# Second half's feed-forward input: 17 of 22 tile pairs as Strassen's 2x2 block product with blocks of 256 tokens, the operand normalised behind the merge

## The chip, the cores and the metric

The kernel runs on one core of a Trainium2 chip. The metric is the time of one execution in microseconds on the device; for the kernel before, the median of three runs is given. A core has TensorE (matmuls, in the profile PE, with its weight loads as PEld), VectorE (DVE), ScalarE (ACT), GpSimd (POOL) and SyncE (SP, which here only issues transfers). Each engine works off its own instructions in order and waits on semaphores for the others.

## What is computed

One decoder layer over 1024 tokens of width 1024, in float32: an RWKV-7 time mixing and an indexer-selected sparse attention, merged by sigmoid gates, then a SwiGLU feed-forward and a final RMSNorm. The part that matters here:

```python
merged = g_a * (y_a @ w_o_rwkv) + g_b * (y_b @ w_o_att)
h = h + merged @ w_out
z = rmsnorm(h, norm2_g) @ w_ffn_in          # 1024 -> 2 x 2816
z_gate, z_up = jnp.split(z, 2, axis=-1)
h = h + (jax.nn.silu(z_gate) * z_up) @ w_ffn_out
return rmsnorm(h, normf_g)
```

## The kernel before, in words

Activations lie transposed: 128 channels in the partitions, 512 tokens (one of two halves of the sequence) in the columns, 8 such tiles for the width of 1024. Every large product is made in three terms, to keep float32's precision: weight and activation are split into a high part, rounded to the PE's input type, and a low part, the rest (`split`, L113: ScalarE copies the high part, VectorE subtracts for the low one), and TensorE adds high x high, high x low and low x high. `mm3` (L135) does that for one output tile of 128 channels x 512 tokens: 8 steps along the width x 3 terms = 24 matmuls of 512 columns into one PSUM tile.

The feed-forward has 22 tile pairs: pair J gives 128 channels of the gate and the same 128 of the up branch, 48 matmuls. `ffn` (L1411) works in three groups of 8, 8 and 6 pairs; behind each group `ffn_out` (L1282) multiplies the group's result f by the output weights and adds it to the stream h, which lies in DRAM. In a pair `ffn_in` (L1254) multiplies both results by a row of one over the RMS per token (`row`), makes silu out of a tanh, multiplies gate and up, and splits the result into f's high and low part. The operand z is h times the norm's gain, without the row: so the products can start before the row is known, and the first pair is ordered (`mm3_late`, L1240) so that z's low part comes last.

What sets the order: TensorE's order is as written, by generators that yield a number of matmuls; `pump(n)` (L175) runs n matmuls of filler from the queue `fill`, and `run_over` (L199) runs a generator and pumps where it yields a negative number. All other engines' instructions are put in order by a scheduler at build time, and their waits follow from tiles and buffers. Weights come in tiles of 512 KB by SP's queue into three raw buffers (`wst`), are split (`weights`, L124) into `whi` and `wlo`, two buffers each.

Around the change the main program does the second half's `merge` (L1193: output projections, gates, `w_out`, h, sums of squares), with the last `ffn_out` of the first half as filler (144 matmuls, 40 of them inside the merge), then the second half's `ffn`, inside which the first half's final norm is placed (`norm_out`, L1313), then a closing stage (`finish_out`). `Rms.columns` sums the squares over the partitions by small matmuls, POOL takes a power, `Rms.spread` brings the result back to all partitions by four small matmuls, and `row` copies that from PSUM. PSUM has 3 tiles `acc` and 5 tiles `mix`; scratch tiles `tmp` are 4.

## Time and profile before

| | |
|---|---|
| median of 3 runs | 1733.7 us |
| lowest, highest | 1728.94, 1736.04 us |
| span of the profiled execution (the page gives no other time of it) | 1731.2 us |
| PE busy | 1700.7 us, 98% |
| DVE, ACT, POOL busy | 65%, 49%, 6% |
| second half's feed-forward to the closing stage | from 1358 to about 1697 us of the span |

In the profile a row of a group reads: line, engine, operation, tiles written <- tiles read, shape, count, then busy time and mean duration, then idle time of the engine before these rows with what ended it. In the chain and timeline views the first number is the start in us from the span's start, the second the duration. In the windows view each stretch has its length, then the busy time of PE, PEld, DVE, ACT and POOL with instruction counts, the granted TensorE clock, the DMA share and GB/s.

### The profile page before, as it was taken

What the parts mean: (1) busy time and instruction counts of PE and PEld (TensorE: products, weight loads), DVE (VectorE), ACT (ScalarE), POOL (GpSimd) and SP (SyncE); (2) the same over time, 40 slices, a digit from 0 to 9 for tenths busy, and PEclk for the clock granted to TensorE, in tenths of its full rate; (3) what the DMA queues carried; (4) which work ended last, traced back from release to release, by engine and by line L of the source; (5) the groups of instructions that cost most, each with busy time, mean ns of one, the idle gap of its engine ahead of it and who ended that gap; (6) DMA issues with size and microseconds to landing.
All of it is one profiled execution on the core that took longest, in us unless ns stands there. A gap on an engine that the chain in (4) does not pass through costs nothing.

```text
span 1731.2 us, 26658 instructions
## 1 busy us (share of the span) xinstructions
PE 1700.7 (98%) x10072; PEld 1405.5 (81%) x10072; DVE 1118.3 (65%) x2172; ACT 848.6 (49%) x1631; POOL 104.8 (6%) x127
## 2 busy tenths in 40 slices
PE   8999999999999998999999999999999999999998
PEld 6888888888778777878787888888888888888888
DVE  6789889866568567857776655535565564354364
ACT  6365998553554788655334355433334322232232
POOL 0000000010021101001100311000000000000001
PEclk9999999999999999999999999999999999999999
DMA  5542334536266536644343765164465344434442
GB/s 212 178 135 96 98 98 147 165 102 182 93 198 185 154 108 177 209 125 117 100 126 117 220 161 136 62 210 131 164 207 151 101 156 152 140 97 152 140 122 98
DMA packets 143282, 247.69 MB, mean 143 GB/s; under 512 B 49153, under 2 KB 71361, under 8 KB 143025
## 3 DMA queue, kind: packets, MB, share of 16 engines
q1 hardware_dynamic: 119072, 170.76, 32.2%
q10 hardware_dynamic: 16128, 48.60, 9.0%
q0 software_dynamic: 7952, 26.61, 5.8%
q8 instruction: 80, 1.31, 0.3%
q14 instruction: 50, 0.40, 0.1%
HBM read 192.92 MB, written 53.00 MB: 142 GB/s over the span
## 4 chain that ended last, share of the span: by engine, by line
PE 89%; DVE 5%; DMA 2%; ACT 2%; issue 1%; POOL 1%; SPq 0%; POOLq 0%; ACTq 0%; DVEq 0%
PE acc L140 22%; PE acc L145 22%; PE acc L141 22%; PE acc L158 3%; PE mix L1103 2%; PE mix L1079 2%; PE mix L944 2%; PE mix L1093 2%; DVE wlo L115 1%; PE mix L140 1%; PE mix L141 1%; PE mix L145 1%; PE acc L1247 1%; PE mix L829 1%; PE mix L699 1%
## 5 line engine op out<-in xcount | busy, mean ns | idle before, releaser
L115 DVE TENSOR_TENSOR wlo<-wst,whi 128x1024 fp32r<-128x1024 f32 (+1 forms) x221 | 268.8, 1218 | 270.3 <-PE acc L145 130.9
L114 ACT ACTIVATE whi<-wst 128x1024 fp32r<-128x1024 f32 (+1 forms) x221 | 231.7, 1049 | 228.5 <-PE acc L141 172.2
L140 PE MATMUL acc<-zhi,whi 128*128 128x512 f32 x672 | 264.7, 394 | 0.0
L141 PE MATMUL acc<-zlo,whi 128*128 128x512 f32 x672 | 262.0, 390 | 0.0
L145 PE MATMUL acc<-zhi,wlo 128*128 128x512 f32 x672 | 170.4, 392 | 0.0
L140 PEld LDWEIGHTS acc<-zhi,whi 128*128 128x128 f32 x672 | 126.2, 188 | 26.9 <-issue 1.7
L141 PEld LDWEIGHTS acc<-zlo,whi 128*128 128x128 f32 x672 | 126.3, 188 | 24.8
L145 PEld LDWEIGHTS acc<-zhi,wlo 128*128 128x128 f32 x672 | 124.7, 188 | 25.5 <-issue 0.7
L140 PE MATMUL acc<-u1hi,whi 128*128 128x512 f32 x320 | 128.4, 401 | 0.0
L141 PE MATMUL acc<-u1lo,whi 128*128 128x512 f32 x320 | 125.5, 392 | 0.0
L140 PE MATMUL acc<-u0hi,whi 128*128 128x512 f32 (+1 forms) x320 | 122.8, 386 | 0.0
L141 PE MATMUL acc<-u0lo,whi 128*128 128x512 f32 (+1 forms) x320 | 121.3, 382 | 0.0
L140 PE MATMUL acc<-fhi,whi 128*128 128x512 f32 x234 | 91.9, 393 | 0.1
L141 PE MATMUL acc<-flo,whi 128*128 128x512 f32 x234 | 91.2, 390 | 0.0
L114 ACT ACTIVATE fhi<-tmp 128x512 fp32r<-128x512 f32 x44 | 27.8, 631 | 114.5 <-DVE tmp L1279 114.5
L145 PE MATMUL acc<-u1hi,wlo 128*128 128x512 f32 x320 | 81.8, 395 | 0.0
L145 PE MATMUL acc<-u0hi,wlo 128*128 128x512 f32 (+1 forms) x320 | 78.6, 384 | 0.0
L1084 ACT ACTIVATE L<-L,mx 128x128 f32<-128x128 f32 (+7 forms) x64 | 49.6, 774 | 45.8 <-DVE mx L1081 45.4
L994 ACT ACTIVATE junkl<-kept,z 128x1024 int8<-128x1024 int16 (+1 forms) x64 | 69.4, 1084 | 4.7 <-DVE kept L963 4.4
L1276 ACT ACTIVATE tmp<-tmp 128x512 f32<-128x512 f32 x44 | 27.8, 631 | 88.8 <-DVE tmp L1275 88.8
L140 PEld LDWEIGHTS acc<-u1hi,whi 128*128 128x128 f32 x320 | 60.3, 189 | 12.7 <-issue 0.9
L140 PEld LDWEIGHTS acc<-u0hi,whi 128*128 128x128 f32 x320 | 60.2, 188 | 11.9 <-issue 0.4
(368 smaller groups left out, 3390.8 us busy)
## 6 DMA issues: line engine op xcount, KB each, us to landing
wst<-in_w_ffn_in SPq DMA_DIRECT2D x72, 512.0 KB, 3.7
wst<-in_w_in ACTq DMA_DIRECT2D x36, 512.0 KB, 4.5
wst<-in_w_in SPq DMA_DIRECT2D x27, 512.0 KB, 3.8
wst<-in_w_fo SPq DMA_DIRECT2D x25, 512.0 KB, 4.2
k<-d_k POOLq DMA_DIRECT2D x24, 512.0 KB, 8.2
h<-in_xT SPq DMA_DIRECT2D x32, 256.0 KB, 5.6
d_g<-tmp ACTq DMA_DIRECT2D x32, 256.0 KB, 3.6
tmp<-d_g SPq DMA_DIRECT2D x32, 256.0 KB, 3.6
```

The costliest lines, as they stand in the source:

```text
L114: A.activation(hi, x, AF.Copy)
L115: V.tensor_tensor(lo, x, hi.bitcast(F32), op=ALU.subtract)
L140: T.matmul(ps, whi[:, wk + k, :], ahi[:, ak + k, tok], start=k == 0, stop=False)
L141: T.matmul(ps, whi[:, wk + k, :], alo[:, ak + k, tok], start=False, stop=False)
L145: T.matmul(ps, wlo[:, wk + k, :], ahi[:, ak + k, tok], start=False, stop=k == nk - 1)
L158: T.matmul(ps, w[:, k, :], a[:, k, tok], start=k == 0 and j == 0, stop=k == nk - 1 and j == 2)
L944: T.matmul(ps[:, :w], iq[:, h, :], ik[:, i, c:c + w], start=i == 0, stop=i == 1)
L994: A.activation(junka[:, :n], y, AF.Sign, bias=z[:, i:i + 1], accum_out=cnt[:, i:i + 1])
L1079: T.matmul(ps[:, :w], q[bi // 2][:, e, bi % 2 * 128:bi % 2 * 128 + 128], k[:, i, e, c:c + w], start=i == 0, stop=i == 1)
L1084: A.activation(L[:, :n], L[:, :n], AF.Exp, scale=-1.0, bias=last, accum_out=sm[:, bi, e:e + 1])
L1093: T.transpose(ps[:, j * 128:(j + 1) * 128], L[:, (c + j) * 128:(c + j + 1) * 128], ident)
L1103: T.matmul(py[64 * e:64 * e + 64, bi * 128:(bi + 1) * 128], v[:, j, 64 * e:64 * e + 64], pts[e][j // 4][:, j % 4, :], start=j == b, stop=j ...
```

## The change

Pairs 3 to 19 of the second half are computed by a 2x2 block product with seven products instead of eight (Winograd's form of Strassen's scheme). The 2x2 block matrix of weights has the gate and the up tile as rows and the two halves of the width (512 each) as columns; that of z has the two halves of the width as rows and the two halves of the tokens (256 each) as columns. One product is 4 steps x 3 terms = 12 matmuls of 256 columns, so a pair has 84 of them instead of 48 of 512 columns.

- `operands` makes z with gain and row in it, behind the merge, splits it, and makes four sums and differences of z's blocks (t1 to t4) with their high and low parts, once for all pairs.
- `prepare` makes, for each pair, four sums of weight blocks (`raw`), and splits these, the gate tile and half of the up tile; its steps are written between the products of the pair ahead. `raw` and the split sums (`bhi`, `blo`) have two buffers each, in a new pool that lies where the first half's tiles lay.
- `pair` writes the seven products: three accumulate further in a PSUM tile after an engine has read it. The seventh product of a pair (`last_block`) is written after four products of the next pair, or at once at a group's end.
- The merge of the second half no longer makes z; sums of squares, row and z follow it, with the 104 matmuls of filler spread between. Pairs 0 to 2, 20 and 21 are as before, without the multiplication by the row. `norm_out` comes 50 matmuls into the feed-forward instead of 100.

In the program's new order, line numbers of helpers are two higher than before (L115 is L117). Three places. First, ScalarE between the merge and the feed-forward, before (L273 is the copy of the row, L114 with `whi` and 768 columns the filler's weights, with 1024 the feed-forward's):

```order
L114 ACTIVATE whi<-wst 128x1024 [waits DMAHW1_49,PE_49,Activation_49]
L114 ACTIVATE whi<-wst 128x1024 [waits DMAHW2_49,PE_49,Activation_49]
L273 ACTIVATE row<-mix 128x512 [waits PE_49]
L1276 ACTIVATE tmp<-tmp 128x512 [waits DVE_49]
L114 ACTIVATE whi<-wst 128x1024 [waits DMAHW3_49,PE_49,Activation_49]
L114 ACTIVATE fhi<-tmp 128x512 [waits DVE_49]
```

and now (L275 is the copy of the row, L248 the squares, L116 `zhi` the high part of z):

```order
L116 ACTIVATE whi<-wst 128x768 [waits DMAHW0_49,PE_49]
L248 ACTIVATE tmp<-h 128x512 [waits DVE_49]
L116 ACTIVATE whi<-wst 128x768 [waits DMAHW2_49,PE_49,Activation_49]
L275 ACTIVATE row<-mix 128x512 [waits PE_49]
L116 ACTIVATE zhi<-h 128x512 [waits DVE_49]
L248 ACTIVATE tmp<-h 128x512 [waits DVE_49]
L116 ACTIVATE whi<-wst 128x768 [waits DMAHW4_49,PE_49,Activation_49]
L116 ACTIVATE zhi<-h 128x512 [waits DVE_49] x2
```

The copy of the row stood behind the first pair's weights; it now stands behind the filler's third last weights, and z's high parts follow it.

Second, VectorE there, before (L1307 adds the filler's result, L247 the squares, L256 is the step of the norm, L1275 to L1279 work on the first pair's result):

```order
L1307 TENSOR_TENSOR h<-h,acc 128x512 [waits DMASW1_49]
L247 TENSOR_TENSOR sacc<-sacc,tmp 128x512 [waits Activation_49]
L256 TENSOR_SCALAR rs<-mix 128x4 [waits PE_49]
L115 TENSOR_TENSOR wlo<-wst,whi 128x1024 [waits DMAHW1_49,Activation_49]
L115 TENSOR_TENSOR wlo<-wst,whi 128x1024 [waits DMAHW2_49,DVE_49,Activation_49]
L1275 TENSOR_TENSOR tmp<-acc,row 128x512 [waits Activation_49]
L1277 SCALAR_TENSOR_TENSOR tmp<-tmp 128x512 [waits Activation_49]
L1278 SCALAR_TENSOR_TENSOR tmp<-acc,row 128x512 [waits DVE_49,PE_49]
L1279 TENSOR_TENSOR tmp<-tmp 128x512 [waits DVE_49]
```

and now (L1313 and L249 for the filler, L1436 multiplies h by gain and row):

```order
L258 TENSOR_SCALAR rs<-mix 128x4 [waits PE_49]
L1313 TENSOR_TENSOR h<-h,acc 128x512 [waits DMASW4_49]
L249 TENSOR_TENSOR sacc<-sacc,tmp 128x512 [waits Activation_49]
L117 TENSOR_TENSOR wlo<-wst,whi 128x768 [waits DVE_49,DMAHW2_49,PE_49,Activation_49]
L1436 SCALAR_TENSOR_TENSOR h<-h,par,row 128x512 [waits DMAHW7_49,Activation_49]
L1313 TENSOR_TENSOR h<-h,acc 128x512 [waits DMASW5_49]
L1436 SCALAR_TENSOR_TENSOR h<-h,par,row 128x512 [waits DMAHW1_49]
L117 TENSOR_TENSOR zlo<-h,zhi 128x512 [waits Activation_49]
L249 TENSOR_TENSOR sacc<-sacc,tmp 128x512 [waits Activation_49]
```

The multiplications by the row and z's low parts stand between the filler's own steps now, eight of each.

Third, VectorE in one pair, before (one pair's steps and the splits of two weight tiles):

```order
L115 TENSOR_TENSOR wlo<-wst,whi 128x1024 [waits DMAHW0_49,PE_49,Activation_49]
L1278 SCALAR_TENSOR_TENSOR tmp<-acc,row 128x512 [waits DVE_49]
L1279 TENSOR_TENSOR tmp<-tmp 128x512 [waits DVE_49]
L115 TENSOR_TENSOR flo<-tmp,fhi 128x512 [waits Activation_49]
L115 TENSOR_TENSOR wlo<-wst,whi 128x1024 [waits DMAHW4_49,PE_49,Activation_49]
L1275 TENSOR_TENSOR tmp<-acc,row 128x512
L1277 SCALAR_TENSOR_TENSOR tmp<-tmp 128x512 [waits Activation_49]
```

and now, from a pair's third product to its sixth (L1466 to L1469 are sums of weights for the next pair, L1521, L1535, L1542 take products out of PSUM, L1504 and L1505 belong to the last product of the pair ahead, L1537 is the gate, `wlo` and `blo` are low parts of the next pair's weights):

```order
L1521 TENSOR_TENSOR tmp<-tmp,mix 128x256 [waits PE_49,Activation_49]
L1468 TENSOR_TENSOR raw<-raw,wst 128x512 [waits DVE_49]
L1505 SCALAR_TENSOR_TENSOR tmp<-m_13456,tmp 128x256
L1469 TENSOR_TENSOR raw<-raw,wst 128x512 [waits DVE_49]
L117 TENSOR_TENSOR wlo<-wst,whi 128x1024
L117 TENSOR_TENSOR blo<-raw,bhi 128x1024 [waits PE_49,Activation_49]
L1504 SCALAR_TENSOR_TENSOR tmp<-mix,tmp 128x256
L1535 TENSOR_TENSOR tmp<-tmp,acc 128x256 [waits PE_49]
L117 TENSOR_TENSOR blo<-raw,bhi 128x1024 [waits Activation_49]
L117 TENSOR_TENSOR flo<-tmp,fhi 128x512 [waits Activation_49]
L1537 SCALAR_TENSOR_TENSOR tmp<-tmp 128x512 [waits Activation_49]
L1542 TENSOR_TENSOR m_13579<-mix,m_13579 128x256 [waits PE_49]
```

Between a result and the steps that wait for ScalarE stand splits of the next pair's weights.

The diff, without the kernel's unchanged helpers:

```diff
--- before.py
+++ after.py
@@ -25,6 +25,8 @@
 HT = 512
 NFF = 22
 GROUPS = [(0, 8), (8, 8), (16, 6)]
+BLOCKED = range(3, 20)
+HB = HT // 2
 TOPK = 256
 C1 = math.exp(-0.5)
 NEG = -3.0e38
@@ -1217,7 +1219,7 @@
         h = zp.tile([128, 8, HT], F32, tag="s0", name="h")
         load_x(half, h, range(8))
         sq = Rms(h)
-        zt = zhi, zlo = act_tiles(zp, "z", ("s1", "s3"))
+        zt = zhi, zlo = act_tiles(zp, "z", ("s1", "s3")) if half == 0 else (None, None)
         pss = []
         if half == 0:
             pss = [acc(), acc()]
@@ -1229,9 +1231,13 @@
                 ps = acc()
                 yield from mm3(ps, weights(ins["w_out"][d]), mt)
             V.tensor_tensor(h[:, d, :], h[:, d, :], ps, op=ALU.add)
-            A.activation(zhi[:, d, :], h[:, d, :], AF.Copy, scale=par[:, P_N2 + d:P_N2 + d + 1])
+            if half == 0:
+                A.activation(zhi[:, d, :], h[:, d, :], AF.Copy, scale=par[:, P_N2 + d:P_N2 + d + 1])
             SY.dma_start(d_h[half][d], h[:, d, :])
             sq.add(d)
+        if half == 1:
+            zs.append(sq)
+            return
         for d in range(8):
             V.scalar_tensor_tensor(zlo[:, d, :], h[:, d, :], par[:, P_N2 + d:P_N2 + d + 1],
                                    zhi[:, d, :].bitcast(F32), op0=ALU.mult, op1=ALU.subtract)
@@ -1417,6 +1423,170 @@
                 yield from ffn_out(half, zp, f, gi)
         kept.append(f)
+    def operands(zp, op, sq, row):
+        h = sq.h
+        z = zhi, zlo = act_tiles(zp, "z", ("s1", "s3"))
+        b = {(r, c): h[:, 4 * r:4 * r + 4, HB * c:HB * c + HB] for r in range(2) for c in range(2)}
+        ts = {i: tuple(op.tile([128, 4, HB], F32R, name=f"t{i}{n}") for n in ("hi", "lo")) for i in range(1, 5)}
+        def steps():
+            for k in range(8):
+                V.scalar_tensor_tensor(h[:, k, :], h[:, k, :], par[:, P_N2 + k:P_N2 + k + 1], row,
+                                       op0=ALU.mult, op1=ALU.mult)
+                split(zhi[:, k, :], zlo[:, k, :], h[:, k, :])
+                yield
+            x, y = b[0, 0], b[0, 1]
+            V.tensor_tensor(x, x, y, op=ALU.subtract)
+            split(*ts[1], x)
+            yield
+            V.tensor_tensor(y, b[1, 1], y, op=ALU.subtract)
+            for i, o in ((2, b[1, 1]), (4, b[1, 0])):
+                V.scalar_tensor_tensor(x, x, -1.0, o, op0=ALU.mult, op1=ALU.subtract)
+                split(*ts[i], x)
+                yield
+            split(*ts[3], y)
+            yield
+        return z, ts, steps()
+    def ffn_blocked(zp, z, ts, steps, wr, kept):
+        zb = {(r, c): tuple(x[:, 4 * r:4 * r + 4, HB * c:HB * c + HB] for x in z) for r in range(2) for c in range(2)}
+        def prepare(J, out):
+            hi, lo = (wr[0].tile([128, 5, 4, 128], F32R, tag=f"b{n}", name=f"b{n}", bufs=2) for n in ("hi", "lo"))
+            raw = wr[0].tile([128, 4, 4, 128], F32, tag="raw", name="raw", bufs=2)
+            def steps():
+                g, u = (raw_weights(ins["w_ffn_in"][2 * J + i]) for i in range(2))
+                for i, a, b in ((0, u[:, 0:4], u[:, 4:8]), (3, g[:, 0:4], u[:, 0:4])):
+                    V.tensor_tensor(raw[:, i], a, b, op=ALU.add)
+                    yield
+                V.tensor_tensor(raw[:, 1], raw[:, 0], g[:, 0:4], op=ALU.add)
+                V.tensor_tensor(raw[:, 2], raw[:, 1], g[:, 4:8], op=ALU.add)
+                yield
+                for i in (0, 2):
+                    split(hi[:, i:i + 2], lo[:, i:i + 2], raw[:, i:i + 2])
+                    yield
+                gs = weights(None, st=g, rush=False)
+                yield
+                split(hi[:, 4], lo[:, 4], u[:, 4:8])
+                w = [tuple(x[:, 4 * i:4 * i + 4] for x in gs) for i in range(2)]
+                out.extend(w + [(hi[:, i], lo[:, i]) for i in range(5)])
+                while True:
+                    yield
+            return steps()
+        def product(ps, w, a, opens=False):
+            (whi, wlo), (ahi, alo) = w, a
+            for k in range(4):
+                T.matmul(ps, whi[:, k, :], ahi[:, k, :], start=opens and k == 0, stop=False, skip_group_check=True)
+                T.matmul(ps, whi[:, k, :], alo[:, k, :], start=False, stop=False, skip_group_check=True)
+            for k in range(4):
+                T.matmul(ps, wlo[:, k, :], ahi[:, k, :], start=False, stop=k == 3, skip_group_check=True)
+        ready, nxt, prev = {}, [iter(())], []
+        def other(J):
+            if J in BLOCKED:
+                ready[J] = []
+                nxt[0] = prepare(J, ready[J])
+            else:
+                nxt[0] = iter(())
+        def last_block():
+            x, w, m5, t, j, f = prev.pop()
+            product(x, w, ts[4])
+            V.scalar_tensor_tensor(t[:, :HB], x, -0.5, t[:, :HB], op0=ALU.mult, op1=ALU.mult)
+            V.scalar_tensor_tensor(t[:, HB:], m5, -0.5, t[:, HB:], op0=ALU.mult, op1=ALU.mult)
+            split(f[0][:, j, :], f[1][:, j, :], t)
+        def pair(J, j, f, ends):
+            a11, a12, s1, s2, s4, s3, a22 = ready.pop(J)
+            x, y, p = mix()[:, :HB], acc()[:, :HB], mix()[:, :HB]
+            c, m5 = tmp(), wr[1].tile([128, HB], F32, tag="m5", name="m5", bufs=2)
+            product(x, a11, zb[0, 0], True)
+            A.activation(c[:, :HB], x, AF.Copy)
+            next(nxt[0], None)
+            yield 6
+            product(y, s1, ts[1], True)
+            A.activation(m5, y, AF.Copy)
+            next(nxt[0], None)
+            yield 6
+            product(p, a12, zb[1, 0], True)
+            V.tensor_tensor(c[:, :HB], c[:, :HB], p, op=ALU.add)
+            next(nxt[0], None)
+            yield 6
+            product(x, s2, ts[2])
+            A.activation(c[:, HB:], x, AF.Copy)
+            next(nxt[0], None)
+            yield 6
+            if prev:
+                last_block()
+                yield 6
+            t = tmp()
+            def low():
+                product(y, s4, zb[1, 1])
+                V.tensor_tensor(c[:, HB:], c[:, HB:], y, op=ALU.add)
+                A.activation(t, c, AF.Tanh, scale=0.5)
+                V.scalar_tensor_tensor(t, t, 1.0, c, op0=ALU.add, op1=ALU.mult)
+                next(nxt[0], None)
+            def high():
+                product(x, s3, ts[3])
+                V.tensor_tensor(m5, x, m5, op=ALU.add)
+                next(nxt[0], None)
+            for step in ((high, low) if ends else (low, high)):
+                step()
+                yield 6
+            for _ in range(2):
+                next(nxt[0], None)
+            prev.append((x, a22, m5, t, j, f))
+            if ends:
+                last_block()
+                yield 6
+        for gi, (g0, gn) in enumerate(GROUPS):
+            f = act_tiles(zp, "f", ("s2", "s0"))
+            for j in range(gn):
+                J = g0 + j
+                if J in BLOCKED:
+                    other(J + 1 if j < gn - 1 else -1)
+                    yield from pair(J, j, f, j == gn - 1 or J + 1 not in BLOCKED)
+                    continue
+                if J + 1 in BLOCKED:
+                    other(J + 1)
+                pss = [acc(), acc()]
+                for i, ps in enumerate(pss):
+                    for n in mm3(ps, weights(ins["w_ffn_in"][2 * J + i]), z):
+                        yield n
+                    for _ in range(4):
+                        next(nxt[0], None)
+                    next(steps, None)
+                t = tmp()
+                A.activation(t, pss[0], AF.Tanh, scale=0.5)
+                V.scalar_tensor_tensor(t, t, 1.0, pss[0], op0=ALU.add, op1=ALU.mult)
+                V.scalar_tensor_tensor(t, pss[1], 0.5, t, op0=ALU.mult, op1=ALU.mult)
+                split(f[0][:, j, :], f[1][:, j, :], t)
+            if gi < len(GROUPS) - 1:
+                done, left = 0, 24 * gn
+                for n in ffn_out(1, zp, f, gi):
+                    yield n
+                    if done < left - 48 <= done + n:
+                        other(g0 + gn)
+                    elif done >= left - 48:
+                        next(nxt[0], None)
+                    done += n
+                for _ in range(8):
+                    next(nxt[0], None)
+        kept.append(f)
     def chain(*gens):
         for g in gens:
             yield from g
@@ -1503,14 +1673,28 @@
     sb.close()
     (sz1, zp1), z1, f1, sq0 = opened("right", "zp1"), [], [], []
     fill.append(ffn_out(0, zp0, f0[0], 2, sq0))
+    sop, op = opened("right", "op")
     run_over(merge(1, zp1, z1))
+    pump(14)
+    z1[0].columns()
+    pump(14)
+    row = z1[0].row()
+    pump(4)
+    z, ts, steps = operands(zp1, op, z1[0], row)
+    for _ in range(8):
+        next(steps)
+        pump(9)
     run(*fill)
-    fill.append(ffn(1, zp1, z1, f1))
-    pump(100)
+    wr = [None, op]
+    fill.append(ffn_blocked(zp1, z, ts, steps, wr, f1))
+    pump(50)
     run_over(norm_out(0, sq0[0]))
+    sz0.close()
+    sw, wr[0] = opened("left", "wr")
     run(*fill)
-    sz0.close()
+    sw.close()
     finish_out(1, zp1, f1[0])
+    sop.close()
     sz1.close()
```

## Prediction

> **What bounds the kernel now.** I read the page first: the span, the busy shares, the chain that ended last.
>
> ```profile
> span 1731.2 us, 26658 instructions
> PE 1700.7 (98%) x10072; PEld 1405.5 (81%) x10072; DVE 1118.3 (65%) x2172; ACT 848.6 (49%) x1631; POOL 104.8 (6%) x127
> ...
> PE 89%; DVE 5%; DMA 2%; ACT 2%; issue 1%; POOL 1%; SPq 0%; POOLq 0%; ACTq 0%; DVEq 0%
> ```
>
> TensorE is 98% busy and 89% of the chain. Then the windows view, for some four tile pairs of the second half's first group:
>
> ```profile
> 1400.00:1448.00 48.00, 48.00 (x213) 39.75 (x212) 26.64 (x33) 15.65 (x19) 0.00 (x0) 1.00 0.38 123
> ```
>
> TensorE never pauses there, at granted clock 1.00; VectorE has 26.64 of 48 us (55%), ScalarE 15.65. So a matmul less is time less, as long as VectorE, which gets the new work, keeps up. Since busy matmuls overlap, the price of one is the step between starts, not its duration. The chain of waits gives it for 512 columns:
>
> ```profile
> 1403.52 1.81 PE acc L145 x8
> 1408.96 1.81 PE acc L145 x8
> 1414.40 1.81 PE acc L145 x8
> ```
>
> Same point of each 24-matmul product: 5.44 us apart, 0.2267 us a matmul. The same precision at 256 columns, each with its own weight load, stands in the timeline at the start of the program:
>
> ```profile
> 32.10 0.28 PE L140 MATMUL mix<-u0hi,whi 128*128 128x256 f32 x1
> 32.22 0.28 PE L141 MATMUL mix<-u0lo,whi 128*128 128x256 f32 x1
> 32.34 0.28 PE L140 MATMUL mix<-u0hi,whi 128*128 128x256 f32 x1
> ```
> ```profile
> 32.11 0.19 PEld L141 LDWEIGHTS mix<-u0lo,whi 128*128 128x128 f32 x1
> 32.22 0.19 PEld L140 LDWEIGHTS mix<-u0hi,whi 128*128 128x128 f32 x1
> 32.34 0.19 PEld L141 LDWEIGHTS mix<-u0lo,whi 128*128 128x128 f32 x1
> ```
>
> 0.120 us a step, loads keeping pace: 0.0067 us more than half of 0.2267.
>
> **The change, part by part. (1) The products.** A pair had 48 matmuls of 512 columns: 48 x 0.2267 = 10.88 us. It gets 7 products of 12 at 256 columns: 84 x 0.120 = 10.08. One product in eight is saved (1.36), and 0.56 goes back because short steps cost more. 17 pairs x 0.80 = **13.6 us off**.
>
> The Trainium skill (TensorE: Matmul & The Clock Gate, Back-to-back issue gap) gives warm steps of N/2.4 + 2.5 ns, 109 at 256 columns and 216 at 512; by it a pair would go from 10.36 to 9.17 us and 17 pairs would save some 20 us, an estimate. Both rows above are 11 ns longer than that rule, so the sum stays with the rows.
>
> **(2) VectorE inside a pair.** Steps of VectorE, again start to start, from its timeline:
>
> ```profile
> 1307.38 1.23 DVE L115 TENSOR_TENSOR wlo<-wst,whi 128x1024 fp32r<-128x1024 f32 x1 [1.61 <-PE acc L145]
> 1308.52 0.68 DVE L1231 TENSOR_TENSOR h<-h,acc 128x512 f32<-128x512 f32 x1
> ...
> 1332.27 0.69 DVE L247 TENSOR_TENSOR sacc<-sacc,tmp 128x512 f32<-128x512 f32 x1 [1.31 <-ACT tmp L246]
> 1332.88 2.07 DVE L1236 SCALAR_TENSOR_TENSOR zlo<-h,par,zhi 128x512 fp32r<-128x512 f32 x3
> 1334.87 0.95 DVE L115 TENSOR_TENSOR wlo<-wst,whi 128x768 fp32r<-128x768 f32 x1
> 1335.73 0.68 DVE L1231 TENSOR_TENSOR h<-h,acc 128x512 f32<-128x512 f32 x1
> ...
> 1374.39 0.69 DVE L1278 SCALAR_TENSOR_TENSOR tmp<-acc,row 128x512 f32<-128x512 f32 x1
> 1375.12 0.69 DVE L1279 TENSOR_TENSOR tmp<-tmp 128x512 f32<-128x512 f32 x1
> ...
> 1721.95 0.41 DVE L1393 TENSOR_TENSOR hT<-hT,acc 128x256 f32<-128x256 f32 x1
> 1722.28 0.61 DVE L1330 SCALAR_TENSOR_TENSOR h<-h,par,mix 128x384 f32<-128x384 f32 x1
> ```
>
> So 1024 columns 1.14, 768 0.86, 512 0.60, with a per-partition scalar 0.66, 256 from PSUM 0.33, and 0.13 more where the next row waits for this one's result. One pair now carries four weight sums (2.40), three low parts of 1024 (3.42) and one of 512 (0.60), five 256-column steps (1.65), the gate (0.60) and f's low part (0.60): 9.27, with three dependent neighbours 9.7 us. That is under 10.08, but by 4%. Order matters then: the rows of VectorE show the scheduler filling each wait (low parts of the next pair stand between the last product's result and the gate). The tightest hand-over: the split weights have two buffers that are freed whole, so the next pair's may be written once the previous pair's last product is done, 5 products = 7.20 us into a pair. Then a ScalarE copy, one VectorE row perhaps ahead (1.14), and the low part (1.14). The copy:
>
> ```profile
> L114 ACT ACTIVATE whi<-wst 128x1024 fp32r<-128x1024 f32 x70 | 74.3, 1061 | 121.6 <-PE acc L141 97.1 <-PE acc L158 13.2 <-PE acc L1251 8.3
> ...
> L114 ACT ACTIVATE whi<-wst 128x768 fp32r<-128x768 f32 x6 | 5.1, 845 | 7.2 <-PE acc L141 4.6 <-issue 2.1 <-ACT tmp L246 0.5
> ...
> L273 ACT ACTIVATE row<-mix 128x512 f32<-128x512 f32 x1 | 0.6, 579 | 0.0
> ```
>
> 7.2 + 1.06 + 1.14 + 1.14, some 10.6; the next pair wants it with its second product's low terms, at 10.08 + 1.44 + 0.96 = 12.5. Near 2 us to spare; I take **0**, and bound it by case B below. ScalarE's own rows in a pair (three copies of 1.06, five shorter) come to some 6 us.
>
> **(3) The start: z waits for the row of norms.** Before, the feed-forward began on raw h and the norm came later. Count from the merge's last matmul as 0. There are 104 matmuls of filler (23.6 us), and inside them now the columns and the spread, which the old chain had a little later:
>
> ```profile
> 1358.05 6.35 PE acc L1247 x28
> 1364.40 0.79 PE mix L253 x8
> ...
> 1369.89 0.89 PE mix L266 x8
> ```
>
> 0.79 and 0.89, the same in both. So TensorE reaches the feed-forward at 25.3 and wants the last piece of z's low part 15 matmuls later, at 28.7. POOL's power fits the 14 matmuls (3.2 us) left for it:
>
> ```profile
> 1365.47 1.03 POOL L259 TENSOR_TENSOR rs<-rs,mhalf 128x4 f32<-128x4 f32 x1 [122.81 <-DVE rs L256]
> ```
>
> But ScalarE's copy of the row stands behind a whi whose buffer frees when the filler's fourth product ends: 3.17 + 0.79 + 3.17 + 0.89 + 0.91 = 8.9. Copy 0.85, VectorE's low part 0.86: the first multiply by the row starts near 10.8. From it to the last piece VectorE has, in the order shown: 8 multiplies (5.3), 8 low parts of z (4.8), 9 steps of the filler's sums and squares (5.4), two low parts of 768 (1.7), two of 1024 (2.3), the first block difference (1.1): 20.6, with 0.4 waiting 31.8. TensorE waits 31.8 - 28.7 = **3.1 us**. Nothing else can run then: its queue is in written order. Bounds: 0 if the row is early enough, 5.5 with VectorE's durations (0.09 more on 27 rows). The four operand sums and the first pair's weights follow with 28 us of rows and some 5 of waits (2.3 for the first half's spread, the rest for weight buffers and for the first half's eight stores, whose memory the new pool takes). They arrive near 65.3, where TensorE wants them at 65.4: I take 0, at most 2.
>
> **(4) At nothing:** weight loads are as many bytes as before; the low part of f at a group's end has 35 matmuls (7.9 us) of the next product over it; the closing stage is untouched.
>
> **Sum**: 1731.2 - 13.6 + 3.1 = 1720.7 for the profiled execution, which was 2.5 us under the median of the three runs (1733.7): **1723.2 us**.
>
> **The rivals. B: VectorE sets the pace.** Were its durations the steps, a pair is 4 x 0.69 + 3 x 1.23 + 3 x 0.69 + 5 x 0.41 = 10.6, with the dependent ones 11.0: 0.5 to 0.9 over TensorE. 14 pairs run beside a preparation (4, 7 and 3 in the groups); with 2.5 us to spare at each group's start 0.9 costs 1.1 + 3.8 + 0.2, 0.5 costs 1.0; the start 2.4 more. 1726.6 to 1730.7, say 1728.6. For it: 96% load; against: each pair of rows above starts 0.08 before the other ends.
>
> The Trainium skill (VectorE: DVE Perf Modes, The DRAIN you can't avoid) says that the next operation does not start until the pipe is empty; that would be case B's arithmetic, and the rows at 1307.38 and 1308.52 disagree.
>
> **C: the loads (slower).** Of three raw-weight buffers a pair holds two; the second load of the pair after next waits for the gate weights' low part, and VectorE's sums wait in order for that load. The loop is landing + 2 sums, p-add, sum, step, sum, low part (1.20 + 0.33 + 0.73 + 0.33 + 0.73 + 1.14 = 4.5). The view of the load's line from 1340 to 1700 us:
>
> ```profile
> DMA to landing us min/median/max: 3.1/3.6/5.1
> ```
>
> 3.6 + 4.5 = 8.1, hidden. It shows from a landing of 5.6 and outweighs the gain from 6.3; at 7.0 a pair is 11.5, so 14 x 0.65 - 3 x 0.8 + 3.1 = +9.8 us, 1743.5. Against it: no load above 5.1.
>
> **D: no stall at the start**, and steps of 0.118: 84 x 0.118 = 9.9, 17 x 0.97 = 16.5 off, 1717.2. For it: a little, since the rows above stand at 0.120. That the blocks are not built as told I exclude: 1428 matmuls of 256 columns stand in TensorE's new order.
>
> **How the numbers follow.** A 0.57 (own range 1719 to 1727), B 0.24, C 0.09, D 0.10. Half a percent, 8.7 us, is about what can be told here: the line is 1725.0. A lies below it in 0.45, D wholly, B in 0.03: faster 0.58. C is slower: 0.09. The rest, 0.33, is no change. The range runs from 1716 (under D by the spread of runs) to 1736 (over B, short of C).
>
> **What would show it.** Steps of 0.120 in the blocked products, and a pair every 10.08 us; TensorE idle some 3 us at the first tile, ended by VectorE's low part of z, and hardly anywhere else; VectorE near 95% between pairs. Wrong would be: waits of TensorE at each pair for blo (B), VectorE waiting for wst inside the groups (C), steps over 0.125.

## The result, and the profile after

The changed kernel took 1719.2 us (median of 4 runs, 1716.4 to 1722.3) beside 1731.3 for the kernel before: ratio 0.9932, 95% interval 0.9907 to 0.9957. Timed twice more in 12 runs each, on two chips, beside the kernel before on the same chip, it gave 0.9973 (0.9958 to 0.9988) and 0.9967 (0.9956 to 0.9979). It is faster each time; by 0.7% first, by 0.3% in the two longer series. The median of all 28 runs is 1723.7 us; the forecast was 1723.2. That these two agree to 0.5 us is in part luck: the forecast set out from 1733.7 us for the kernel before, and the median of its 47 runs timed beside the experiments is 1730.2. So the whole time fell by 6.5 us, where 10.5 were forecast.

Whole times are too coarse to judge the steps by. Up to the last matmul of the second half's merge TensorE has the same matmuls in the same order in both kernels; of the work of ScalarE and VectorE only z's first high and low parts (seven and two rows) are gone there, and GpSimd's is the same. And yet that stretch lasted 1327.7 to 1338.6 us in 14 profiles. So the steps are judged by what comes behind it: from the start of the merge's last matmul to the end of the span. TensorE's timeline has that matmul as the last of a group, before and after (start, duration, line, out<-in, count):

```profile
1332.73 1.75 PE L145 MATMUL acc<-mhi,wlo 128*128 128x512 f32 x7
```
```profile
1326.33 1.75 PE L147 MATMUL acc<-mhi,wlo 128*128 128x512 f32 x7
```

The seventh starts 6 x 0.2267 us behind the first: 1334.1 and 1327.7. With spans of 1731.2 and 1714.6 us, 397.1 us follow it before and 386.9 after, **10.1 us less**; the forecast of this stretch was 10.5 less. The other 6.4 us of the two profiles' difference lie ahead of the change.

The page of the changed kernel:

```profile
span 1714.6 us, 28086 instructions
PE 1686.0 (98%) x10684; PEld 1421.2 (83%) x10684; DVE 1191.1 (69%) x2314; ACT 892.7 (52%) x1720; POOL 104.2 (6%) x127
...
PE 89%; DVE 4%; ACT 3%; DMA 2%; issue 1%; POOL 1%; ACTq 0%; POOLq 0%; DVEq 0%; SPq 0%
```

TensorE still bounds the whole; VectorE went from 65 to 69%. The chain of waits shows the blocks' step, and TensorE's timeline the same point of three neighbouring pairs:

```profile
1403.97 0.48 PE mix L1490 x4
1405.41 0.48 PE mix L1490 x4
```
```profile
1411.48 0.28 PE L1487 MATMUL acc<-t1hi,bhi 128*128 128x256 f32 x1
1421.57 0.28 PE L1487 MATMUL acc<-t1hi,bhi 128*128 128x256 f32 x1
1431.64 0.28 PE L1487 MATMUL acc<-t1hi,bhi 128*128 128x256 f32 x1
```

A product of 12 each 1.44 us (0.120 a step) and a pair each 10.08, as forecast. The windows view of those three pairs that also prepare the next one (third figure: VectorE busy), of the last pair of that group, which prepares none, and of six pairs of the second group:

```profile
1401.40:1431.64 30.24, 30.24 (x254) 30.24 (x253) 29.15 (x47) 16.99 (x28) 0.00 (x0) 1.00 0.39 124
1431.64:1441.72 10.08, 10.08 (x86) 10.08 (x85) 6.29 (x12) 3.80 (x7) 0.00 (x0) 1.00 0.58 190
1495.36:1555.83 60.47, 60.47 (x507) 60.47 (x506) 52.00 (x83) 34.07 (x54) 0.00 (x0) 1.00 0.31 97
```

In the first group VectorE is busy 29.15 / 3 = 9.72 us a pair, 96%, and TensorE never stops. Its timeline has four low parts of gate weights in these three pairs; without the fourth (1.14 us) VectorE's work is 9.3 us a pair. In the second group it is 52.00 / 6 = 8.67, because only five preparations' weight sums fall into these six pairs: the group entered with one made ahead. And the start, in the timelines of TensorE and VectorE:

```profile
1357.65 0.51 PE L142 MATMUL acc<-zhi,whi 128*128 128x512 f32 x1 [0.73 <-ACT zhi L116]
1359.32 0.50 PE L143 MATMUL acc<-zlo,whi 128*128 128x512 f32 x1 [1.17 <-DVE zlo L117]
1359.66 2.01 PE L147 MATMUL acc<-zhi,wlo 128*128 128x512 f32 x8
```
```profile
1338.37 0.74 DVE L1436 SCALAR_TENSOR_TENSOR h<-h,par,row 128x512 f32<-128x512 f32 x1
...
1356.19 0.74 DVE L1436 SCALAR_TENSOR_TENSOR h<-h,par,row 128x512 f32<-128x512 f32 x1
...
1357.45 1.22 DVE L1441 TENSOR_TENSOR h<-h 128x1024 f32<-128x1024 f32 x1
1358.59 0.68 DVE L117 TENSOR_TENSOR zlo<-h,zhi 128x512 fp32r<-128x512 f32 x1
```

The idle times in brackets are counted from the modelled ends of matmuls; start to start TensorE loses 0.89 and 1.45, together 2.34 us. The view of waits from 1325 to 1680 us has these two, 0.2 us in the first blocked pair, and nothing else.

### The profile page after: what moved, and what is told of

It is laid out like the page before. It is cut to its first block, busy times and chain, and to the rows that moved or that the text cites. A ratio compares the mean times of both kernels' runs of the same rounds, so it can differ in the third digit from the quotient of the medians.

```text
span 1714.6 us, 28086 instructions
## 1 busy us (share of the span) xinstructions
PE 1686.0 (98%) x10684; PEld 1421.2 (83%) x10684; DVE 1191.1 (69%) x2314; ACT 892.7 (52%) x1720; POOL 104.2 (6%) x127
## 4 chain that ended last, share of the span: by engine, by line
PE 89%; DVE 4%; ACT 3%; DMA 2%; issue 1%; POOL 1%; ACTq 0%; POOLq 0%; DVEq 0%; SPq 0%
PE acc L142 19%; PE acc L143 19%; PE acc L147 19%; PE acc L160 4%; PE mix L1487 2%; PE mix L1490 2%; PE mix L1488 2%; PE mix L1105 2%; PE mix L1081 2%; PE mix L1095 2%; PE mix L946 2%; DMA wst<-in_w_ffn_in 1%; PE mix L142 1%; PE mix L143 1%; PE mix L147 1%
## 5 line engine op out<-in xcount | busy, mean ns | idle before, releaser
L117 DVE TENSOR_TENSOR wlo<-wst,whi 128x1024 fp32r<-128x1024 f32 (+1 forms) x204 | 249.5, 1224 | 179.2 <-PE acc L147 79.8
L116 ACT ACTIVATE whi<-wst 128x1024 fp32r<-128x1024 f32 (+1 forms) x204 | 213.4, 1047 | 187.3 <-PE acc L143 131.7
L142 PE MATMUL acc<-zhi,whi 128*128 128x512 f32 x416 | 165.7, 398 | 0.7 <-ACT zhi L116 0.7
L143 PE MATMUL acc<-zlo,whi 128*128 128x512 f32 x416 | 162.9, 392 | 1.2 <-DVE zlo L117 1.2
L147 PE MATMUL acc<-zhi,wlo 128*128 128x512 f32 x416 | 107.5, 394 | 0.0
L142 PEld LDWEIGHTS acc<-zhi,whi 128*128 128x128 f32 x416 | 78.4, 188 | 18.1 <-issue 1.7
L143 PEld LDWEIGHTS acc<-zlo,whi 128*128 128x128 f32 x416 | 78.5, 189 | 16.3 <-DVE zlo L117 1.5
L147 PEld LDWEIGHTS acc<-zhi,wlo 128*128 128x128 f32 x416 | 76.9, 189 | 15.6 <-issue 0.7
L143 PEld LDWEIGHTS acc<-u1lo,whi 128*128 128x128 f32 x320 | 60.1, 188 | 11.3
L147 PEld LDWEIGHTS acc<-u1hi,wlo 128*128 128x128 f32 x320 | 58.9, 188 | 12.5 <-issue 0.9
```

The source lines that it names most:

```text
L116: A.activation(hi, x, AF.Copy)
L117: V.tensor_tensor(lo, x, hi.bitcast(F32), op=ALU.subtract)
L142: T.matmul(ps, whi[:, wk + k, :], ahi[:, ak + k, tok], start=k == 0, stop=False)
L143: T.matmul(ps, whi[:, wk + k, :], alo[:, ak + k, tok], start=False, stop=False)
L147: T.matmul(ps, wlo[:, wk + k, :], ahi[:, ak + k, tok], start=False, stop=k == nk - 1)
```

## The experiments

Each kernel's time from the merge's last matmul to the end, read as above:

```
kernel                       merge's last   span     between   waits of TensorE   half-speed steps cost
before                          1334.1     1731.2     397.1          0                 0
the change                      1327.7     1714.6     386.9         3.1                0
  again (e8_again)              1331.2     1718.6     387.4         3.4                0
  a third time (e8_twice)       1336.2     1724.9     388.7         3.3                1.4
no block products (e1)          1338.3     1738.1     399.8         2.5                0
halves (e2)                     1337.6     1749.9     412.3         2.7                1.4
six products (e3_six)           1331.2     1702.3     371.1         8.0                2.8
two sums more (e3_dve_2)        1330.0     1733.9     403.9        12.6                6.3
row 8 matmuls earlier (e4)      1332.3     1716.5     384.2         0.5                0
  again, timed (e4_row5)        1334.8     1718.7     383.9         0.2                0
row 8 matmuls later (e7)        1330.3     1715.3     385.1         1.1                0
operand's last pieces first (e9) 1338.6    1723.0     384.4         0.6                0
pairs 20, 21 too (e5)           1330.7     1723.1     392.4         3.1                -
row earlier, pair 20 too (e6)   1331.3     1714.7     383.4         0.6                0
```

The fifth column adds up, over TensorE's starts up to the last product, all steps that are 0.13 us or more over 0.2267 or 0.120; the sixth the steps of 0.4267 and 0.2135 us that stand in runs.

### The normalisation alone

```diff
-BLOCKED = range(3, 20)
+BLOCKED = range(0)
```

> The change without its block products: the operand is normalised behind the merge, the sums for the blocks are still built, but all 22 pairs run as 48 matmuls of 512 columns. I count from the merge's last matmul to the end of the profile: 397.1 us before, 386.9 with the change. Theory (the gain is the saved product in eight, 17 x 0.80, and the normalisation costs a stall at the start): nothing is gained, the start's wait of 2.3 us stays, 397.1 + 2.5 = 399.6 us, the whole some 2 to 3 us over the kernel before. Rival (part of the gain is the row multiplies that left the pairs): under 397, say 390 to 395.

Measured 399.8, ratio 1.0015 (1.0001 to 1.0029; 1735.7 us, 10 runs). The start's wait is there to the hundredth (0.89 and 1.45), and nothing is gained. The blocks alone are then worth 399.77 - 386.93 = 12.8 us, and 13.4 without the 0.6 us that the first blocked pair waits: 0.79 us a pair.

### The price of a short matmul

```diff
-for n in mm3(ps, weights(ins["w_ffn_in"][2 * J + i]), z):
-    yield n
+w = weights(ins["w_ffn_in"][2 * J + i])
+for a, b in ((0, HB), (HB, HT)) if 3 <= J < 20 else ((0, HT),):
+    yield from mm3(ps[:, a:b], w, z, tok=slice(a, b))
```

on the kernel without block products.

> As the kernel with the normalisation alone, and pairs 3 to 19 run each product as two halves of 256 tokens, 96 matmuls of 256 columns and no block sums. This prices the short matmul by itself. Theory (a step of 0.120 us): 96 x 0.120 - 48 x 0.2267 = +0.64 us a pair, 17 pairs +10.9 us over the kernel with the normalisation alone, some 410 us from the merge's last matmul to the end. Rival, by the rule of the Trainium skill (TensorE: Matmul & The Clock Gate, Back-to-back issue gap): 96 x 0.1092 - 48 x 0.2158 = +0.12 us a pair, +2 us, some 402.

412.3, 12.5 over e1 (1747.2 us, ratio 1.0090, 1.0059 to 1.0122). 8 steps behind the start's wait ran at half speed here and cost 1.6; the rest, 10.9, is 0.64 us a pair. In its timeline:

```profile
1419.86 0.28 PE L142 MATMUL acc<-zhi,whi 128*128 128x256 f32 x1
1419.98 0.28 PE L143 MATMUL acc<-zlo,whi 128*128 128x256 f32 x1
```

0.120 us a step, over all 1632 of them. The formula of the Trainium skill (TensorE: Matmul & The Clock Gate, Back-to-back issue gap), by which 109 ns are worked out here, does not hold for these products; its 2 us would have been missed by 9. That section of the Trainium skill calls it the gap of an isolated matmul and gives some 131 ns at 512 columns for streams with weight loads; the 226.7 ns measured here are longer than that too.

### VectorE's margin, from both sides

The seventh product of each blocked pair, and with it that part of the result, left out:

```diff
 x, w, m5, t, j, f = prev.pop()
-product(x, w, ts[4])
```

> The change with the seventh product of each blocked pair (the block that is taken off the linear half) left out, 12 matmuls of 84; all work of VectorE stays. This part of the result is left out. If TensorE alone set the pace, 17 x 1.44 = 24.5 us would go: 386.9 - 24.5 = 362.4 us from the merge's last matmul to the end. Theory (VectorE needs 9.7 us of the 10.08 in each pair that prepares the next): 14 pairs fall only to 9.7, the three without a preparation by 1.44: 5.3 + 4.3 = 9.6 us off, some 377, with up to 2.5 us of room at the start of each group 370 to 377. Then TensorE waits in the pairs for split weights.

371.1: of the 24.5 us that TensorE no longer works, 15.8 are gained. The three figures that matter are PE, PEld and VectorE, in the first group and in two stretches of two pairs each of the second:

```profile
1403.00:1414.40 11.40, 11.22 (x94) 11.02 (x93) 11.13 (x19) 7.78 (x13) 0.00 (x0) 1.00 0.29 93
1490.10:1507.40 17.30, 17.30 (x147) 17.30 (x146) 17.09 (x26) 9.97 (x17) 0.00 (x0) 1.00 0.40 125
1524.70:1542.00 17.30, 17.30 (x146) 17.30 (x146) 16.92 (x28) 11.33 (x18) 0.00 (x0) 1.00 0.38 130
```
```profile
PE mix L1490 <- DVE wlo L117: 3.0, 1, 3.0
PE mix L1487 <- ACT tmp L1524: 1.6, 4, 0.5
```

VectorE is 98% busy, so it is the next bound; but the second and third group still ran at 8.64 us a pair, TensorE's own pace, where 9.7 was expected. With 9.3 us of work in a pair of 8.64 VectorE must fall behind through a group; it did so without stopping TensorE there. Both groups enter with one preparation's weight sums made ahead (that of the second starts at 1485.3, the group's first pair at 1488.8), and the last pair prepares nothing. Only the first group paid for the lag (3.1 us); in it VectorE comes straight from the operands' sums, with no lead. Each group's last pair waits 0.6 us more, for ScalarE's copy of a result: the product that stood over it is the one left out. The total fell into the expected range, the account within it was wrong for two groups of three.

And more for VectorE:

```diff
 V.tensor_tensor(raw[:, 2], raw[:, 1], g[:, 4:8], op=ALU.add)
+V.tensor_tensor(raw[:, 2], raw[:, 1], g[:, 4:8], op=ALU.add)
+V.tensor_tensor(raw[:, 2], raw[:, 1], g[:, 4:8], op=ALU.add)
```

> The change with one weight sum of each preparation done three times, 1.2 us more on VectorE a pair, same result. Theory (9.7 us of 10.08 in use): 10.9 us a pair, 0.8 over TensorE; 14 pairs would lose 11.8 us, less up to 2.5 us of room at each of three groups: +4 to +12, 391 to 399 us from the merge's last matmul to the end. Rival (the window's 82% for VectorE is right for the pairs, 1.8 us of room in each): nothing changes, 387.

403.9, 17.0 more, and 1735.7 us in the one run: the whole gain is gone. The longer waits account for 9.5 of it; the whole is above the expected 4 to 12. The view of waits (wait, total, times, longest), TensorE's timeline at the longest, and windows of just before, of the wait, behind it, and after that:

```profile
PE mix L1492 <- DVE wlo L117: 9.0, 2, 5.7
```
```profile
1415.49 0.28 PE L1490 MATMUL mix<-zlo,whi 128*128 128x256 f32 x1
1421.49 1.22 PE L1492 MATMUL mix<-zhi,wlo 128*128 128x256 f32 x4 [5.72 <-DVE wlo L117]
1422.51 0.41 PE L1489 MATMUL acc<-t1hi,bhi 128*128 128x256 f32 x1
1422.72 0.41 PE L1490 MATMUL acc<-t1lo,bhi 128*128 128x256 f32 x1
```
```profile
1409.50:1415.40 5.90, 5.90 (x52) 5.90 (x51) 5.17 (x10) 2.67 (x4) 0.00 (x0) 1.00 0.43 151
1415.60:1421.40 5.80, 0.17 (x2) 0.00 (x0) 5.61 (x8) 2.25 (x4) 0.00 (x0) 0.95 0.00 0
1421.50:1427.60 6.10, 6.10 (x28) 6.10 (x29) 3.90 (x6) 1.36 (x3) 0.00 (x0) 0.50 0.52 172
1428.00:1434.00 6.00, 6.00 (x53) 6.00 (x52) 5.96 (x10) 3.62 (x7) 0.00 (x0) 1.00 0.19 49
```

TensorE is not slowed in each pair by VectorE's excess. It stops twice, where a product wants the gate weights' low part and that row stands behind rows of two pairs in VectorE's order (5.9 us, and 3.4 in the second group). But the added work is not the only thing that changed: in the change this row comes once a pair (at 1407.71, 1416.65 and 1426.22), here at 1403.86, 1420.22 and 1422.29. The scheduler wrote another order for the heavier kernel, and two pairs' excess, 2 x (9.3 + 1.2 - 10.08) = 0.8 us, is far less than 5.9. So how much of the 17.0 us is load and how much order is not shown. What nobody expected is the third window: behind the wait TensorE's granted clock is 0.50 for 6 us, with 28 matmuls instead of some 52. Steps of 0.2135 and 0.4267 us cost 6.3 us in this profile.

### Where the start's wait comes from

The row of norms earlier, then later:

```diff
 z1[0].columns()
-pump(14)
+pump(6)      # e7: pump(22)
 row = z1[0].row()
```

> The change with the row of norms spread 8 matmuls of filler earlier (6 instead of 14 between the columns and the spread). Theory (the start stall comes from the first multiply by the row standing at 10.7 us after the merge, behind a spread and a weight copy that are late, while VectorE idles 3.0 us just ahead of it): VectorE's string of rows starts some 2 us sooner, the 2.3 us that TensorE waits for the operand shrinks to 0.3 to 0.6; TensorE may wait 0.4 for the power ahead of the spread. 386.9 - 1.5 = 385.4 us from the merge's last matmul to the end. Rival (the string is paced by the filler's products, whose sums stand between its rows): the wait stays at 2.3, 387.

> The change with the row of norms spread 8 matmuls of filler later (22 instead of 14 between the columns and the spread). Theory (the operand's string on VectorE starts with the row): the start's wait grows from 2.3 to some 4.1 us, and TensorE's steps behind it run at half speed for several us, 0.2 us lost at each step of 512 columns: 386.9 + 1.8 + 1.5 to 5, 390 to 394 us from the merge's last matmul to the end. Rival (paced by the filler's products): the wait stays at 2.3, 387 to 388.5.

Earlier: 384.2, the wait is gone altogether, and at least half of the 0.6 us in the first blocked pair with it. Later: 385.1, outside both forecasts, and the wait is gone there too, down to 0.18 us. So the theory that made both forecasts, that the row's arrival alone sets the wait, is refuted: in e7 the first multiply stood at 11.8 us behind the merge (1342.05), 1.1 later than in the change, and the last low part came earlier all the same. VectorE's timelines, start and end of the string, of e4 and then of e7:

```profile
1340.44 0.75 DVE L1436 SCALAR_TENSOR_TENSOR h<-h,par,row 128x512 f32<-128x512 f32 x1 [1.34 <-ACT row L275]
...
1360.28 0.68 DVE L117 TENSOR_TENSOR zlo<-h,zhi 128x512 fp32r<-128x512 f32 x1
```

```profile
1342.05 1.41 DVE L1436 SCALAR_TENSOR_TENSOR h<-h,par,row 128x512 f32<-128x512 f32 x2
...
1358.58 1.28 DVE L117 TENSOR_TENSOR zlo<-h,zhi 128x512 fp32r<-128x512 f32 x2
1359.78 0.67 DVE L1313 TENSOR_TENSOR h<-h,acc 128x512 f32<-128x512 f32 x1
1360.38 1.21 DVE L1441 TENSOR_TENSOR h<-h 128x1024 f32<-128x1024 f32 x1
```

Between the first multiply and the end of the last low part lie 17.8 us in e7, 20.9 in the change: there two sums and a square of the filler more, and the first block difference (L1441, 1.14), stand in front of the last low part. In e4 the string is 20.5 us, about as long as in the change, but starts at 8.1 instead of 10.7: there it is the earlier row that helps. Both kernels move the spread by 8 matmuls, and the scheduler then wrote another order. To change the order alone, with spread and row where they were:

```diff
 for k in range(8):
+    with tc.high_priority() if k > 5 else nullcontext():
-    V.scalar_tensor_tensor(h[:, k, :], ...)
-    split(zhi[:, k, :], zlo[:, k, :], h[:, k, :])
+        V.scalar_tensor_tensor(h[:, k, :], ...)
+        split(zhi[:, k, :], zlo[:, k, :], h[:, k, :])
     yield
```

> The change with the operand's last two pieces (multiply, high part, low part) given priority; the spread and the row of norms stay at their place on TensorE. VectorE's order then has 10 rows of filler in front of the operand's last low part instead of 13 and the first block difference. Both the earlier and the later row took the wait away, so the theory is now that VectorE's order sets the wait and not the time of the row: 10.7 + 8 multiplies 5.3 + 8 low parts 4.8 + 6 sums and squares 3.6 + 2 low parts of 768 1.7 + 2 of 1024 2.3 = 28.4 us after the merge, as TensorE wants it: a wait of 0 to 0.5 instead of 2.3, 384.5 to 385 us from the merge's last matmul to the end. Rival (the row's time does it): wait 2.3, 387.

384.4, with a wait of 0.25; 1721.0 us, ratio 0.9940 (0.9927 to 0.9953). The row's first multiply starts 10.7 us behind the merge, as in the change, and the last low part at 27.9 instead of 30.9:

```profile
1349.31 1.41 DVE L1437 SCALAR_TENSOR_TENSOR h<-h,par,row 128x512 f32<-128x512 f32 x2
...
1366.53 0.68 DVE L117 TENSOR_TENSOR zlo<-h,zhi 128x512 fp32r<-128x512 f32 x1
1367.13 1.28 DVE L1313 TENSOR_TENSOR h<-h,acc 128x512 f32<-128x512 f32 x2
1368.33 1.22 DVE L1442 TENSOR_TENSOR h<-h 128x1024 f32<-128x1024 f32 x1
```

The row is where it was and TensorE's order is unchanged, so here the order alone (VectorE's, and ScalarE's with it) takes the wait down from 2.3 to 0.25 us. The operand is ready at the start of VectorE's string plus its length, and an earlier start or a shorter string takes the wait away. In us behind the merge, where TensorE wants the last low part at 29.3:

```
                 first multiply   string   last low part done
the change            10.7         20.9          31.6
e4, row earlier        8.1         20.5          28.6
e7, row later         11.8         17.8          29.6
e9, order only        10.7         17.9          28.6
```

### More pairs

```diff
-BLOCKED = range(3, 20)
+BLOCKED = range(3, 22)      # e6: range(3, 21), and pump(6) ahead of the row
```

> The change with the last two pairs, 20 and 21, as block products too, 19 pairs of 22. Theory by the step alone: 2 x 0.80 = 1.6 us less, 385.3 us from the merge's last matmul to the end. Against it stands the closing stage, whose weights take the memory of the blocks' split weights: their copy (0.85) and low part (0.86) can only be written when the last blocked pair is through, so TensorE would wait 1 to 3 us at the closing stage's first product: 386 to 388, no gain.

392.4, 5.5 us worse. The products gained 1.4; the closing stage took 50.2 us instead of 43.3, 6.9 more where 1 to 3 were expected. TensorE's timeline there:

```profile
1674.14 2.41 PE L160 MATMUL acc<-fhi,wf 128*128 128x384 f32 x10 [0.98 <-ACT wf L116]
...
1687.74 0.41 PE L142 MATMUL acc<-fhi,wf 128*128 128x384 f32 x1 [3.56 <-DVE h L1373]
...
1688.47 0.52 PE L143 MATMUL acc<-flo,wf 128*128 128x384 f32 x1
1688.79 0.52 PE L142 MATMUL acc<-fhi,wf 128*128 128x384 f32 x1
```

The first weights' copies were late by 1.0, as thought. The larger part was not foreseen: VectorE's additions that free the result buffers came late too (3.6; that the weights' low parts queued ahead of them are the reason was not tried), and the matmuls behind that wait run at 0.32 us a step, half speed again.

> The earlier row of norms and pair 20 as a block product too, 18 pairs; pair 21 stays whole, so that its 10.9 us lie between the last blocked pair and the closing stage, whose weights take the blocks' memory. Theory: one more saving of 0.80 us, 384.2 - 0.8 = 383.4 us from the merge's last matmul to the end. Rival: the closing stage's memory is free too late even so (with both last pairs in blocks the closing stage took 6.9 us longer), 384 to 390.

With pair 21 left whole: 383.4, as expected; 1716.6 us, ratio 0.9929 (0.9912 to 0.9946). This is the shortest stretch of all kernels with the full result. On the same chip the row moved alone gave

> The kernel with the earlier row of norms again, now timed. One look had 384.2 us from the merge's last matmul to the end, 2.7 under the change. Theory: the gain stands in the whole time too, 1719 - 2.7, some 1716 us, ratio to the kernel before 0.990 to 0.993. Rival: the look was lucky in the pairs and the gain is the start's 2.3 at most, within what the change has.

383.9 us and 1719.0 us, ratio 0.9934 (0.9918 to 0.9951), and the change itself

> The changed kernel itself, beside the others on one chip. Theory: 1716 to 1722 us, ratio to the kernel before near 0.993. In four other profiles with the same 2.3 us wait at the start, three show 8 half-speed steps of TensorE behind it (0.4267 for 0.2267 us) and 1.5 us lost: where this one shows them, it has 388.4 us from the merge's last matmul to the end, otherwise 386.9.

387.4 us and 1725.6 us, ratio 0.9973 (0.9958 to 0.9988). The intervals of both versions lie below that of the change; e6 and e4 cannot be told apart by whole times, only by the 0.5 us behind the merge.

> The changed kernel itself a third time, on another chip. Its ratio to the kernel before was 0.993 and 0.997 so far, while the stretch behind the merge was 386.9 and 387.4 us in both. Theory (the earlier stages, the same instruction for instruction, make the difference from run to run): the stretch is again 387 or, with half-speed steps behind the wait, 388.5, whatever the whole time; ratio between 0.992 and 0.997. Rival (something of the change itself costs more on some chips): the stretch is over 390.

388.7 us, ratio 0.9967 (0.9956 to 0.9979). Here the half-speed steps stand behind the start's wait:

```profile
1367.88 0.55 PE L143 MATMUL acc<-zlo,whi 128*128 128x512 f32 x1 [1.17 <-DVE zlo L117]
1368.23 3.56 PE L147 MATMUL acc<-zhi,wlo 128*128 128x512 f32 x8
```

Eight matmuls take 3.56 us; in the first profile of the change the same eight take 2.01. The stretch behind the merge is the same within 1.8 us in three profiles, so in them nothing of the change costs far more in one series than in another there. Why then did the whole times gain 12 us in the first series and 4 and 6 in the others? Each run's mean granted clock is on record. At an equal clock the change is 8.7 to 10.0 us faster: at 0.996 1721.1 us (mean of 8 runs) beside 1729.8 (21 runs), at 0.994 1725.6 (9) beside 1734.8 (5). But the change's 28 runs had 0.9945 on average, and 0.996 in the first series alone, beside 0.9955 in those 47 of the kernel before. Half-speed steps behind the start's wait are part of that in the third profile; where the rest lies stays open, since runs without a profile show no stretches.

## Why the prediction was right

**(1) The products.** Right. 10.08 us a pair, 0.120 a step; the products' saving read from the trace is 13.4 us for a forecast of 13.6. e2 measured the term that decides, the short step, by itself: 0.64 us a pair for twice as many matmuls of half the length. Had the step followed the formula of the Trainium skill that the prediction names, the gain would have been some 20 us, an estimate from the figures of that section.

**(2) VectorE inside a pair.** Right for the change: no wait of TensorE behind the first blocked pair. That 9.72 us were read where 9.7 was worked out is partly luck: with one low part too many in that window taken off, the work is 9.3, nearer to the sum of the rows (9.27) without its three dependent neighbours. The margin is 0.8 us a pair then, twice what was told, but still thin: with 1.2 us more VectorE work in a pair, and the order that the scheduler then wrote, the gain is gone. Case B named the right engine but not the form of the cost. It spread the excess over pairs and credited 2.5 us of lead to each group; e3_six shows second and third groups that take 0.7 us a pair of excess with no wait for it, and e3_dve_2 two waits at single rows, each paid once more by a slower clock.

**(3) The start.** The time was right, 2.3 us for 3.1; the reason was half right. The first multiply stood at 10.7 us (10.8 forecast), the string from it took 20.9 (20.6 and 0.4 of waiting). TensorE reached the feed-forward at 25.9 us instead of 25.3 and so wanted the last piece 0.6 later: that is most of the difference, and the string's end, 31.6 for 31.8, the rest. The row's copy, which "stands behind a whi", is one of two terms that set the wait (e4); the rows that the scheduler put in between are the other (e9), and e7 had the row later and next to no wait. Both were in the sum, but the order of the rows was taken as given. The operands and the first blocked pair's weights, taken at 0 with 2 as a bound, cost 0.6 to 0.9.

**(4)** Right: the closing stage, counted from the last product of z, took 43.3 us before and after.

**The cases.** C did not come. The view of the weight loads' line from 1340 to 1700 us, after:

```profile
DMA to landing us min/median/max: 3.1/3.6/5.2
```

No load took the 5.6 us from which the case would show. The sign named for it, VectorE waiting for `wst` inside the groups, did appear once in the second group and once in the third (1.9 and 2.2 us), without stopping TensorE:

```profile
1497.64 1.29 DVE L1466 TENSOR_TENSOR raw<-wst 128x512 f32<-128x512 f32 x2 [1.92 <-DMA wst<-in_w_ffn_in]
```

D did not come either: the wait was there and the steps were 0.120; e4 shows what its first half is worth, 2.7 to 3.0 us. Case B's arithmetic rested on one sentence of the Trainium skill (VectorE: DVE Perf Modes, The DRAIN you can't avoid); the same paragraph goes on that a next operation that is not held starts earlier, which is what the rows at 1307.38 and 1308.52 show. The sum missed one thing: what a wait of TensorE costs behind its end, 1.4 us in the third profile of the change and nothing in the first two.

## What to carry to other kernels

Price a replaced matmul by start-to-start steps of the same size in the trace, not by its length: here a block product saves 12.5% of the columns and 7.3% of the time. Work that moved onto a second engine cost nothing here as long as that engine had room over a whole group, not in each step; when the room ends, look for the row that stands last in its written order. When TensorE waits at a seam, read the order of the engine it waits for as well as the time of the producer: three different edits of a few rows were worth more than two further blocked pairs. And compare whole times at an equal granted clock before judging a gain of half a percent.

## What was not expected of the hardware

A wait of TensorE is not over when it ends. In eight profiles with the same wait of 0.89 and 1.45 us at the start, four show 7 to 8 steps of 0.4267 instead of 0.2267 us right behind it, 1.4 to 1.6 us more, and four show none. Behind waits of 3.1, 3.4 and 5.9 us came 15, 25 and 27 slow steps of 0.2135, each time: 1.4, 2.3 and 2.5 us. The windows view shows it as a granted clock of 0.50 (1421.50 to 1427.60 in e3_dve_2) right behind a stretch at 0.95 in which TensorE did nothing.

The granted clock in the traces says why the same wait is followed by slow steps only sometimes. In each of the 14 traces all changes of the clock lie whole multiples of 3.413 us apart, and the half-clock stretches behind these waits last 3.41 or 6.83 us. So the clock changes on a grid that does not start with the wait, and what counts is how much of the wait falls into one interval of it. The windows view by intervals of this grid, the one with the most idle time and the next, for the third profile of the change (slow steps) and the first (none):

```profile
1364.76:1368.18 3.42, 1.52 (x6) 0.73 (x5) 3.42 (x6) 2.10 (x3) 0.00 (x0) 1.00 0.38 150
1368.18:1371.59 3.41, 3.41 (x9) 2.64 (x8) 2.58 (x3) 1.24 (x2) 0.00 (x0) 0.50 0.02 5
```
```profile
1355.57:1358.98 3.41, 1.86 (x7) 0.96 (x6) 3.41 (x6) 1.46 (x3) 0.00 (x0) 1.00 0.52 154
1358.98:1362.39 3.41, 3.07 (x13) 2.55 (x14) 3.41 (x5) 2.57 (x4) 0.00 (x0) 1.00 0.02 5
```

In the four profiles with slow steps 2.1 us or more of the wait (start to start) fall into one interval, and TensorE is busy for 1.51 to 1.65 us of it; in the four others at most 2.0 fall into one, and TensorE is busy for 1.86 or more. The clock of the next interval is 0.50 in all four of the first and 1.00 in all four of the others. Between these figures nothing was measured here, and ahead of the merge, with other matmuls, the clock also fell behind busier intervals; so busy time is not the whole rule.

The Trainium skill (TensorE: Matmul & The Clock Gate, What's actually happening) tells of a clock gate that halves the clock after an idle window of about 3.4 us that runs freely; its next section (Wait — 56ns, not 53.3ns?) gives 426.7 ns for 512 columns at the half clock. The slow steps agree to the digit, and the grid of 3.413 us agrees with a free-running window; but the window need not be idle throughout: 2.1 us of idle time in one were enough here.
